# Second part of a hybrid decoder layer: VectorE sums for left operands, seven raw buffers for right operands

## The chip, the core and the metric

The kernel runs on one core of a Trainium2 chip. The metric is the device time of one execution in microseconds, as the median of several runs. The engines are called as in the profile: PE is TensorE's matmul, PEld its weight load, DVE is VectorE, ACT is ScalarE, POOL is GpSimd, SP is SyncE, which in this kernel issues most of the loads.

## The reference

One decoder layer on 2048 tokens of width 1024, with 16 meta tokens put in front. Two branches, a Mamba-2 scan and a gated linear attention, get their inputs from one projection, and two sigmoid gates merge them:

```python
u = rmsnorm(hres, norm_w)
proj = jnp.einsum('bld,dn->bln', u, w_in)
z, xbc, dt_raw, q, k, v, g_gla, a_lr, merge_g = split_cols(proj, IN_WIDTHS)
...
branches = jnp.stack([y_ssd.astype(y_gla.dtype), y_gla], axis=2)
branch_proj = jnp.einsum('blnc,ncd->blnd', branches, w_branch)
gates = jax.nn.sigmoid(merge_g.reshape(b, l, N_BRANCH, D_MODEL))
merged = jnp.sum(gates * branch_proj, axis=2)
return hres + jnp.einsum('bld,de->ble', merged, w_out)
...
return rmsnorm(h, final_norm_w)[:, N_META:]
```

All tensors are float32. The scans and their projections are the kernel's first part. The second part, which the change concerns, is the gates' projection (`merge_g`), the two branch projections and the output projection, with the final norm.

## The kernel before

*First part*, up to about 1487 us: projections, both scans, the branch outputs `y` and the normed input `u` go to DRAM in blocks.

*Second part*: seven stages, one after the other: gates of the first token block, its two branches, gates of the second block, its two branches, output. Each stage is a product of large matrices done by a Strassen-like scheme (Winograd's form): left and right matrices are cut in quarters, and seven products p = 1 to 7 stand for the eight of the plain way. The gate stages and the output have 8 left blocks n each (56 products), the branch stages 4 (28 products): 280 products in all.

A product (L1044 to L1060) is 12 matmuls of 128x512: four pieces j of the contraction, each done three times, since every operand is split into a high and a low half to keep float32 accuracy (lines L193 to L195: high by high and the two mixed ones). Products are written in the order p = 1, 2, 6, 7, 5, 3, 4, with two n interleaved, so that a pair of n makes a cycle of 14 products.

*Right operands* (28 per stage: 7 p times 4 j). `load_b` loads one from DRAM into a raw tile `br` of the pool `rawb`, which has five buffers, by a DMA on SP's queue (L1011). `prep_b` splits it: ACT copies the high half (L1016), DVE subtracts it to give the low half (L1017); these are the tiles `b`. Three of the seven are sums or differences of quarters that `make_sums` (L84) worked out earlier and stored to DRAM; those for the stages after the first gate stage are worked out inside the gate stages, in 64 instructions on POOL.

*Left operands*. `load_a` loads four quarters of each n into tiles `ar` (pool of eight, L1023 on SP's queue): three at one call, the fourth (a22) at a later call, 1.5 products on. At that call four additions and subtractions on POOL (L1031 to L1034) give the sums `as` and one new `ar`. `prep_a` splits each of the seven into tiles `a`: ACT at L1040, DVE at L1041.

*What a product leaves*. Three PSUM banks are kept going at once per n, named `psa`, `psb`, `psc`. The bank `psa` takes p = 1, 6, 5 and 3 in turn, each added to the last; after p = 1, 6 and 5 ACT copies the bank to a snapshot `sn` (L1057), and PE may not go on in that bank before the copy is done. Between p = 5 and p = 3 of one n lies only one product of the other n. A result is the bank, or a snapshot plus another bank (DVE, L1068). A gate stage then applies tanh (ACT, L1075) and stores; a branch stage multiplies with the gate on DVE and stores or adds in DRAM; the output stage adds the residual (DVE, L1117), squares (ACT, L1121) and, when a row is complete, takes the power -0.5 on POOL (L1129) and scales (DVE, L1132). Stores go by POOL's queue (L991).

*What sets the order*. A table `todo` holds, for each product's number, what is to be emitted after it: left loads 7.5 products before their first use, left splits 5 products before use, the splits of a stage's right operands 12 products ahead of its first product, then one each 0.8 products, and the loads 3.2 products ahead of their split. The order on PE and SP is that of the program. The order on ACT, DVE and POOL is set by a scheduler in the build, which works on a model of time. All queues are in order: an instruction that waits holds those behind it.

Of the kernel before, what the change touches and what calls it, by code (L numbers as in the profile page):

```python
# [7 lines left out]
F32 = mybir.dt.float32  # L8
# [4 lines left out]
ALU = mybir.AluOpType  # L13

P = 128
# [3 lines left out]
BLK = 512  # L19
# [21 lines left out]
def trunk_kernel(ctx: ExitStack, tc: tile.TileContext, xm, xmt, w_feat, w_tok, w_zm, w_br, w_o,  # L41
                 cf32, cmsk, pvec, fnw, hvec, gw2, out):
    nc = tc.nc
# [5 lines left out]
    def mk(pool, shape, dt, tag, **kw):  # L49
        cnt[0] += 1  # L50
        return pool.tile(shape, dt, tag=tag, name=f"{tag}_{cnt[0]}", **kw)
# [24 lines left out]
    def make_sums(pool, tag, nb, braw, sums, j, c, store):  # L76
        cs = slice(c * HB, (c + 1) * HB)
        pair = [mk(pool, [P, 512], F32, tag, bufs=nb).rearrange("p (i c) -> p i c", i=2) for _ in range(2)]
        for r, (k, t) in zip((t[:, i] for t in pair for i in range(2)), ((0, 1), (0, 0), (1, 1), (1, 0))):
            nc.sync.dma_start(r, braw(4 * k + j, t)[:, cs])  # L80
        yield
        (b12, b11), (b22, b21) = [(t[:, 0], t[:, 1]) for t in pair]
        for o, x, y in ((b11, b12, b11), (b12, b22, b12), (b22, b22, b11), (b21, b21, b22)):
            nc.gpsimd.tensor_tensor(o, x, y, op=ALU.subtract)  # L84
        if store is None:
            for dst, src in zip(sums, pair):
                late_store(dst[j][:, :, cs], src, 2)
            return
        yield
        yield  # L90
        for dst, src in zip(sums, pair):
            store.dma_start(dst[j][:, :, cs], src)
# [3 lines left out]
    def late_store(dst, src, lag=1):  # L96
        stores.setdefault(step_no[0] + lag, []).append((dst, src))
# [295 lines left out]
    def new_block(b, u):  # L393
        o = Block()
        o.b, o.u = b, u
        o.m0 = META if b == 0 else 0
        o.tt = o.m0 + BLK
        o.segs_all = [(0, o.tt // 2), (o.tt // 2, o.tt // 2)] if b == 0 else [(0, BLK)]
        o.segs_real = [(o.m0, BLK)]
        o.starts = [o.m0 + c * P for c in range(NCH)]  # L400
        o.chunks = ([(0, META)] if o.m0 else []) + [(a, P) for a in o.starts]
        o.ci0 = 1 if o.m0 else 0
        o.nck = len(o.chunks)
        for nm in ("tkd", "tkc", "ntc", "wde", "ecu", "dec"):
            setattr(o, nm, mk(bpool, [P, 5, NH], F32, nm, bufs=1))
        o.cumd = mk(dpool, [NH, BLK], F32, "cumd")
        o.g_all = mk(bpool, [P, GH, META + BLK], F32, "g_all")
        o.both = None
        if o.m0:
            o.both = mk(early, [P, KT, 2 * META], F32R, "both", bufs=1)  # L410
            for i in range(2):
                nc.gpsimd.tensor_copy(o.both[:, :, i * META:(i + 1) * META], u[i][:, :, :META].bitcast(F32))
        o.alr = mk(bpool, [P, 5, 48], F32, "alr")
        o.mov = lambda kt, a, n: tuple(t[:, kt, a:a + n] for t in u)
        return o
# [515 lines left out]
    def beside_unit(key):  # L931
        for j in range(4):
            for c in range(2):
                yield from make_sums(early, "wr", NWR, *sums[key], j, c, nc.sync)

    with tc.manual_schedule(engines={mybir.EngineType.PE, mybir.EngineType.SP}):
        for b in range(nblk):
            o = new_block(b, next_u[b])
# [25 lines left out]
    def pool2(name, bufs, **kw):  # L964
        return second.enter_context(tc.tile_pool(name=name, bufs=bufs, reuse_waits="tile", **kw))

    npl = pool2("rawb", 5)
# [4 lines left out]
    bpl = pool2("bops", 4)  # L972
    opl = pool2("outs", 1)
    spl = pool2("small", 4)
    pa = pool2("pa", 3, space=bass.MemoryType.PSUM)
    pc2 = pool2("pc2", 2, space=bass.MemoryType.PSUM)
    pb = pool2("pb", 3, space=bass.MemoryType.PSUM)
# [6 lines left out]
    store = late_store  # L984
# [11 lines left out]
    class Stage:  # L996
# [9 lines left out]
        def load_b(self, p, j):  # L1006
            src = {1: lambda j: self.braw(j, 0), 2: lambda j: self.braw(4 + j, 0), 3: lambda j: self.braw(4 + j, 1),
                   4: lambda j: self.sums[1][j][:, 1], 5: lambda j: self.sums[0][j][:, 1],
                   6: lambda j: self.sums[1][j][:, 0], 7: lambda j: self.sums[0][j][:, 0]}[p]
            raw = self.braws[p, j] = mk(npl, [P, BLK], F32, "br")  # L1010
            nc.sync.dma_start(raw, src(j))  # L1011

        def prep_b(self, p, j):
# [6 lines left out]
        def load_a(self, n):  # L1020
            def raw(i, j):
                t = mk(rpl, [P, 4, P], F32, "ar")
                nc.sync.dma_start(t, self.araw(n, i, j))  # L1023
                return t

            if n not in self.a:
                self.a[n] = raw(0, 0), raw(0, 1), raw(1, 0)
                return
            (a11, a12, a21), a22 = self.a[n], raw(1, 1)
            s1, s2, s4 = [mk(spl2, [P, 4, P], F32, "as") for _ in range(3)]  # L1030
            nc.gpsimd.tensor_tensor(s1, a21, a22, op=ALU.add)  # L1031
            nc.gpsimd.tensor_tensor(s2, s1, a11, op=ALU.subtract)
            nc.gpsimd.tensor_tensor(a21, a11, a21, op=ALU.subtract)
            nc.gpsimd.tensor_tensor(s4, a12, s2, op=ALU.subtract)  # L1034
            self.a[n] = {1: a11, 2: a12, 3: s4, 4: a22, 5: s1, 6: s2, 7: a21}

        def prep_a(self, n, p):
# [118 lines left out]
    def at(pos, fn):  # L1156
        pos = max(pos, -1)
        todo.setdefault(int(pos // 1), []).append((pos, len(todo), fn))
# [7 lines left out]
    for si, st in enumerate(stages):  # L1166
        for q in range(28):
            p, j = PS[q // 4], q % 4
            pos = begins[si] - 12 + 0.8 * q if si else -0.99 + 0.2 * (q // 4) if q < 16 else 2 * (q // 4 - 4)
            if si or p > 1:  # L1170
                at(pos - (3.2 if si else 0.1), lambda st=st, p=p, j=j: st.load_b(p, j))
            at(pos, lambda st=st, p=p, j=j: st.prep_b(p, j))
    for i, (st, n, p) in enumerate(order):
        if p in USES and st.fetch:
# [3 lines left out]
    begun_at = [begins[3 * s] for s in range(nsb)]  # L1178
    spots = [g + 9 + 5 * k for g in begun_at for k in range(8)]
    late_sums = [make_sums(opl, "io", 8, *sums[key], j, c, None) for key in late for j in range(4) for c in range(2)]  # L1180
    for pos, gen in zip(spots, late_sums):
        for k in range(2):
# [104 lines left out]
```

## Time and profile before

| | us |
|---|---|
| median of three runs | 2296.2 |
| the runs | 2296.17, 2296.2, 2300.63 |
| span of the profiled execution | 2298.3 |
| of this: PE busy | 2223.2 |
| DVE busy | 1646.5 |
| ACT busy | 1119.4 |
| POOL busy | 789.6 |
| second part, 1487 to 2298: PE busy | 774.0 |
| DVE, ACT, POOL busy there | 604.0, 395.4, 421.2 |

The profiled execution lies 2.1 us above the median. The stages of the second part begin at 1487.4, 1656.4, 1733.0, 1815.6, 1976.1, 2052.2 and 2130.7 us; the last product ends at 2286.8.

How to read the views that follow: in a row of the timeline stand start and length in us, engine, line, operation, tiles (out<-in), a count, and in brackets the time that the engine had been idle and what ended it. A row of waits gives the engine and line that waits, what it waits for, and us in total, times, longest. A row of a group gives busy us and mean ns, then idle time just before it.

### The profile page before, as it was taken

Reading aid. Unit: us, or ns where it says so; the run is one execution under the profiler, and the core shown is the slowest. Engines: PE = TensorE matmul, PEld = TensorE weight load, DVE = VectorE, ACT = ScalarE, POOL = GpSimd, SP = SyncE. Lnnn points to the kernel's source line nnn. Section 1 sums busy time; section 2 is a strip of 40 time slices with the busy share of each in tenths; the row PEclk is TensorE's granted clock in tenths of the full one; section 3 lists DMA queues with packets and bytes.
Section 4 is the critical chain, followed back from the end, with each engine's and each line's share of the span. In section 5 each row is a group of like instructions: output and inputs, shape, how many; then the busy total and the mean of one; then the engine's idle time right before and its main releaser. Section 6 shows DMA issues by size and latency. Waiting matters only on the chain.

```text
span 2298.3 us, 36496 instructions
## 1 busy us (share of the span) xinstructions
PE 2223.2 (97%) x12599; PEld 1938.7 (84%) x12599; DVE 1646.5 (72%) x3108; ACT 1119.4 (49%) x2508; POOL 789.6 (34%) x869
## 2 busy tenths in 40 slices
PE   6899999999999999999999999989999999999998
PEld 6899888888889889888988898868787788788786
DVE  5787767687765687775678656687778855788775
ACT  5565554463444454444445434554644545454443
POOL 3344533122221122212212100158535476535452
PEclk9999999999999999999999999999999999999999
DMA  7767866667886676886677654466767866679653
GB/s 254 232 221 245 296 211 208 211 193 246 267 264 208 205 225 208 272 278 206 203 215 230 215 184 149 149 221 205 264 233 223 249 216 213 233 251 252 182 185 110
DMA packets 281866, 507.51 MB, mean 221 GB/s; under 512 B 27104, under 2 KB 134880, under 8 KB 281680
## 3 DMA queue, kind: packets, MB, share of 16 engines
q1 hardware_dynamic: 217232, 413.76, 55.7%
q0 software_dynamic: 17568, 50.87, 7.3%
q10 hardware_dynamic: 46880, 40.54, 5.4%
q8 instruction: 99, 1.62, 0.3%
q14 instruction: 87, 0.71, 0.1%
HBM read 357.87 MB, written 147.19 MB: 220 GB/s over the span
## 4 chain that ended last, share of the span: by engine, by line
PE 73%; DVE 9%; DMA 9%; issue 4%; ACT 3%; POOL 2%; SPq 1%; ACTq 0%; POOLq 0%; DVEq 0%
PE pj L193 13%; PE pj L195 13%; PE pj L194 13%; PE psa L193 4%; PE psa L195 4%; PE psa L194 4%; DMA br<-br_t 2%; PE psb L195 2%; PE psb L193 2%; PE psb L194 2%; DVE b L1017 2%; PE pc L619 2%; PE pc L789 2%; PE pc L889 1%; PE pc L620 1%
## 5 line engine op out<-in xcount | busy, mean ns | idle before, releaser
L193 PE MATMUL pj<-u,whl 128*128 128x512 f32 (+1 forms) x1184 | 445.5, 376 | 9.4 <-ACT acc L529 4.5
L195 PE MATMUL pj<-u,whl 128*128 128x512 f32 (+1 forms) x1184 | 429.5, 363 | 0.0
L194 PE MATMUL pj<-u,whl 128*128 128x512 f32 (+1 forms) x1184 | 428.9, 362 | 0.0
L193 PE MATMUL pj<-whl,u 128*128 128x256 f32 (+1 forms) x992 | 288.8, 291 | 2.8 <-ACT u L261 2.2
L195 PE MATMUL pj<-whl,u 128*128 128x256 f32 (+1 forms) x992 | 282.4, 285 | 0.2 <-DVE u L266 0.2
L194 PE MATMUL pj<-whl,u 128*128 128x256 f32 (+1 forms) x992 | 282.1, 284 | 0.0
L193 PE MATMUL psa<-b,a 128*128 128x512 f32 x640 | 252.3, 394 | 18.1 <-ACT sn L1057 17.9
L193 PEld LDWEIGHTS pj<-u,whl 128*128 128x128 f32 x1184 | 223.6, 189 | 47.2 <-ACT acc L529 5.4
L195 PEld LDWEIGHTS pj<-u,whl 128*128 128x128 f32 x1184 | 223.2, 188 | 35.6
L194 PEld LDWEIGHTS pj<-u,whl 128*128 128x128 f32 x1184 | 223.9, 189 | 33.1
L194 PE MATMUL psa<-b,a 128*128 128x512 f32 x640 | 250.2, 391 | 0.9 <-DVE b L1017 0.9
L195 PE MATMUL psa<-b,a 128*128 128x512 f32 x640 | 250.5, 391 | 0.0
L84 POOL TENSOR_TENSOR wr<-wr 128x256 f32<-128x256 f32 x80 | 64.2, 803 | 428.8 <-DMA wr<-u 163.4
L181 POOL TENSOR_TENSOR whl<-wr,whl 128x512 fp32r<-128x512 f32 (+1 forms) x100 | 138.3, 1389 | 187.2 <-ACT whl L180 154.8
L1041 DVE TENSOR_TENSOR a<-ar,a 128x512 fp32r<-128x512 f32 x160 | 157.3, 993 | 61.9 <-ACT a L1040 61.4
L1017 DVE TENSOR_TENSOR b<-br,b 128x512 fp32r<-128x512 f32 x196 | 159.1, 833 | 49.1 <-ACT b L1016 48.8
L193 PEld LDWEIGHTS pj<-whl,u 128*128 128x128 f32 x992 | 189.8, 191 | 4.5 <-ACT u L261 2.3
L195 PEld LDWEIGHTS pj<-whl,u 128*128 128x128 f32 x992 | 189.8, 191 | 0.8 <-DVE u L266 0.8
L194 PEld LDWEIGHTS pj<-whl,u 128*128 128x128 f32 x992 | 189.9, 191 | 0.4
L1016 ACT ACTIVATE b<-br 128x512 fp32r<-128x512 f32 x196 | 120.1, 628 | 125.2 <-DMA br<-br_t 53.6
L533 DVE SCALAR_TENSOR_TENSOR acc<-cin,hcw,acc 128x512 f32<-128x512 f32 (+1 forms) x192 | 161.3, 840 | 11.4 <-ACT acc L529 9.3
L193 PEld LDWEIGHTS psa<-b,a 128*128 128x128 f32 x640 | 120.9, 189 | 49.3 <-ACT sn L1057 24.7
(297 smaller groups left out, 5064.5 us busy)
## 6 DMA issues: line engine op xcount, KB each, us to landing
whl<-k_s SPq DMA_DIRECT2D x96, 512.0 KB, 4.4
whl<-k_g SPq DMA_DIRECT2D x96, 512.0 KB, 4.2
whl<-k_v SPq DMA_DIRECT2D x48, 512.0 KB, 4.0
whl<-k_z SPq DMA_DIRECT2D x36, 512.0 KB, 4.1
wr<-in_w_feat SPq DMA_DIRECT2D x64, 256.0 KB, 4.4
k_s<-whl SPq DMA_DIRECT2D x32, 512.0 KB, 3.8
cb<-cumd ACTq DMA_DIRECT2D x64, 256.0 KB, 5.8
k_g<-whl SPq DMA_DIRECT2D x32, 512.0 KB, 3.8
```

The source lines that it names most:

```text
L84: nc.gpsimd.tensor_tensor(o, x, y, op=ALU.subtract)
L181: nc.gpsimd.tensor_tensor(hl[:, 1], raw, hl[:, 0].bitcast(F32), op=ALU.subtract)
L193: nc.tensor.matmul(ps, sh, mh, start=first, stop=False, **kw)
L194: nc.tensor.matmul(ps, sh, ml, start=False, stop=False, **kw)
L195: nc.tensor.matmul(ps, sl, mh, start=False, stop=last, **kw)
L533: nc.vector.scalar_tensor_tensor(acc, cin[:, k:k + tt], hcw[:, ti, k:k + 1], acc, op0=ALU.mult, op1=ALU.add)
L619: nc.tensor.matmul(py[:, h * 64:(h + 1) * 64], dm[:, h], xdt[:, h], start=True, stop=True)
L620: nc.tensor.matmul(py[:, 256:512], cf[:, a:a + P], s_ssd[:, g], start=True, stop=True)
L789: nc.tensor.matmul(ps[:, r * P:(r + 1) * P], kq[:, 2 * r * P:(2 * r + 1) * P], kq[:, (2 * r + 1) * P:(2 * r + 2) * P], start=True, stop=True)
L1016: nc.scalar.activation(t[:, 0], raw, AF.Copy)
L1017: nc.vector.tensor_tensor(t[:, 1], raw, t[:, 0].bitcast(F32), op=ALU.subtract)
L1041: nc.vector.tensor_tensor(t[:, 1], src, t[:, 0].bitcast(F32), op=ALU.subtract)
```

## The change

Three edits, all in the second part. The four sums of `load_a` and the 64 late differences of `make_sums` (where `store is None`) move from POOL to DVE. The pool of raw right operands becomes a ring of seven, as a second pool of two stands beside the five. And the loads of right operands are emitted 4.8 products ahead of their split, not 3.2. Lines from L974 on move by 6 in the changed file (the sums L1031 to L1034 are L1037 to L1040 there, the DVE splits L1023 and L1047, the copies L1063, the adds L1074).

```diff
-            nc.gpsimd.tensor_tensor(o, x, y, op=ALU.subtract)
+            (nc.vector if store is None else nc.gpsimd).tensor_tensor(o, x, y, op=ALU.subtract)
...
+    npl2 = pool2("rawb2", 2)
+    taken = [0]
+
+    def raw_b():
+        taken[0] += 1
+        return mk(npl2 if taken[0] % 7 > 4 else npl, [P, BLK], F32, "br")
...
-            raw = self.braws[p, j] = mk(npl, [P, BLK], F32, "br")
+            raw = self.braws[p, j] = raw_b()
             nc.sync.dma_start(raw, src(j))
...
-            nc.gpsimd.tensor_tensor(s1, a21, a22, op=ALU.add)
-            nc.gpsimd.tensor_tensor(s2, s1, a11, op=ALU.subtract)
-            nc.gpsimd.tensor_tensor(a21, a11, a21, op=ALU.subtract)
-            nc.gpsimd.tensor_tensor(s4, a12, s2, op=ALU.subtract)
+            nc.vector.tensor_tensor(s1, a21, a22, op=ALU.add)
+            nc.vector.tensor_tensor(s2, s1, a11, op=ALU.subtract)
+            nc.vector.tensor_tensor(a21, a11, a21, op=ALU.subtract)
+            nc.vector.tensor_tensor(s4, a12, s2, op=ALU.subtract)
...
-                at(pos - (3.2 if si else 0.1), lambda st=st, p=p, j=j: st.load_b(p, j))
+                at(pos - (4.8 if si else 0.1), lambda st=st, p=p, j=j: st.load_b(p, j))
```

DVE has 224 instructions more and POOL 224 fewer; the counts on the other engines stay. The order of the first part is the same on every engine.

On SP, at the end of the second gate stage (about 1945 us; `br` are raw right operands of the next stage, `ar` left quarters), the order before:

```order
L1011 DMA br_21448<-br_t_3_196 128x512
L1023 DMA ar_21466<-in_w_br 128x512
L1011 DMA br_21481<-br_t_0_189 128x512
L1023 DMA ar_21483<-in_w_br 128x512
L1023 DMA ar_21485<-in_w_br 128x512
L1023 DMA ar_21487<-in_w_br 128x512
L1023 DMA ar_21506<-in_w_br 128x512
L1011 DMA br_21521<-br_t_1_190 128x512
L1011 DMA br_21541<-br_t_2_191 128x512
L1011 DMA br_21549<-br_t_3_192 128x512
```

and now:

```order
L1017 DMA br_21420<-br_t_3_196 128x512
L1029 DMA ar_21425<-in_w_br 128x512
L1029 DMA ar_21427<-in_w_br 128x512
L1029 DMA ar_21429<-in_w_br 128x512
L1017 DMA br_21431<-br_t_0_189 128x512
L1017 DMA br_21455<-br_t_1_190 128x512
L1029 DMA ar_21473<-in_w_br 128x512
L1017 DMA br_21485<-br_t_2_191 128x512
L1029 DMA ar_21490<-in_w_br 128x512
L1029 DMA ar_21492<-in_w_br 128x512
L1029 DMA ar_21494<-in_w_br 128x512
L1029 DMA ar_21513<-in_w_br 128x512
```

The right operands br_t_1_190 and br_t_2_191 stand ahead of the last four left quarters, where they stood behind them.

On ACT, at the end of the first branch stage (about 1722 us; L1016, now L1022, are splits of right operands, L1057, now L1063, the copies of a bank after p = 5 of two n), the order before:

```order
L1040 ACTIVATE a_19377<-ar_19056 128x512
L1040 ACTIVATE a_19419<-ar_19316 128x512
L1016 ACTIVATE b_3396_19473<-br_19380 128x512
L1057 ACTIVATE sn_19362<-psa_19151 128x512
L1040 ACTIVATE a_19448<-ar_19385 128x512
L1016 ACTIVATE b_3400_19498<-br_19425 128x512
L1057 ACTIVATE sn_19403<-psa_19174 128x512
```

and now:

```order
L1046 ACTIVATE a_19384<-ar_19059 128x512
L1022 ACTIVATE b_3398_19480<-br_19332 128x512
L1022 ACTIVATE b_3401_19503<-br_19355 128x512
L1046 ACTIVATE a_19426<-ar_19323 128x512
L1022 ACTIVATE b_3405_19528<-br_19390 128x512
L1063 ACTIVATE sn_19369<-psa_19158 128x512
L1046 ACTIVATE a_19455<-ar_19392 128x512
L1022 ACTIVATE b_3409_19549<-br_19432 128x512
L1063 ACTIVATE sn_19410<-psa_19181 128x512
```

Each copy stands behind two later splits of right operands than before.

On DVE, in the first gate stage (about 1563 us; L1068, now L1074, is the add of a snapshot and a bank), the order before:

```order
L1041 TENSOR_TENSOR a_17973<-ar_17683,a_17973 128x512
L1041 TENSOR_TENSOR a_18010<-ar_17922,a_18010 128x512
L1068 TENSOR_TENSOR sn_17960<-sn_17960,psb_17906 128x512
L1041 TENSOR_TENSOR a_18028<-ar_17976,a_18028 128x512
L1068 TENSOR_TENSOR sn_17994<-sn_17994,psb_17928 128x512
```

and now:

```order
L1047 TENSOR_TENSOR a_17976<-ar_17686,a_17976 128x512
L1047 TENSOR_TENSOR a_18013<-ar_17925,a_18013 128x512
L1037 TENSOR_TENSOR as_18006<-ar_17983,ar_18004 128x512
L1038 TENSOR_TENSOR as_18007<-as_18006,ar_17979 128x512
L1039 TENSOR_TENSOR ar_17983<-ar_17979,ar_17983 128x512
L1040 TENSOR_TENSOR as_18008<-ar_17981,as_18007 128x512
L1074 TENSOR_TENSOR sn_17963<-sn_17963,psb_17909 128x512
L1047 TENSOR_TENSOR a_18031<-ar_17979,a_18031 128x512
L1074 TENSOR_TENSOR sn_17997<-sn_17997,psb_17931 128x512
```

The four sums, of which the first reads the fourth quarter (ar_18004), stand between the splits and the add.

## The prediction

> **What bounds the kernel now.** I read the busy times by stretch of the second part first, then the waits there, then one stall in three timelines. In the stretches the columns are: length, then busy time and count of PE, PEld, DVE, ACT and POOL, granted clock, DMA share, GB/s.
>
> ```profile
> 1487.00:1580.00 93.00, 83.91 (x362) 67.45 (x361) 75.39 (x76) 51.30 (x97) 57.30 (x61) 0.96 0.65 217
> 1640.00:1700.00 60.00, 57.75 (x254) 47.17 (x253) 44.49 (x57) 30.23 (x54) 29.84 (x29) 1.00 0.65 226
> 1700.00:1760.00 60.00, 59.13 (x259) 47.97 (x258) 51.38 (x65) 32.18 (x58) 24.39 (x22) 1.00 0.78 255
> 1760.00:1820.00 60.00, 57.15 (x244) 46.51 (x243) 49.08 (x62) 25.90 (x46) 30.04 (x25) 0.97 0.86 237
> 1940.00:2000.00 60.00, 54.31 (x233) 44.41 (x232) 43.01 (x55) 32.10 (x59) 22.71 (x22) 0.97 0.72 241
> 2000.00:2060.00 60.00, 60.00 (x267) 49.65 (x266) 49.30 (x63) 29.10 (x51) 25.64 (x24) 1.00 0.72 247
> 2120.00:2180.00 60.00, 55.56 (x243) 45.03 (x242) 48.57 (x69) 29.60 (x60) 28.40 (x26) 1.00 0.69 194
> ```
>
> TensorE is the bound: a full stretch holds 267 matmuls in 60 us, one every 0.2247 us, and a product of 12 takes 2.7 us. Only fewer gaps can shorten the part; the change touches no matmul. The stretches from 1640, 1700, 1760, 1940 and 2120 lack 13, 8, 23, 34 and 24 matmuls, 102 in all or 23 us; each holds the end of one stage and the start of the next. The first stretch could hold 93 / 0.2247 = 414 and has 362: 11.7 us at the start. Together some 35 us, which is the most that this change can win.
>
> ```profile
> PE psa L193 <- ACT sn L1057: 17.9, 13, 5.7
> PE psc L194 <- DVE b L1017: 6.7, 2, 4.0
> ACT b L1016 <- DMA br<-br_t: 53.6, 32, 6.7
> ACT b L1016 <- DMA br<-gate_t: 27.6, 18, 4.2
> ACT b L1016 <- DMA br<-out_t: 19.2, 9, 6.3
> ```
>
> These are the waits (total us, times, longest). At stage ends PE waits for no operand: it waits for ACT's copy of a PSUM bank (L1057), because the same bank must take the next product (p=3 after p=5 of the other n, one product later). ACT in turn stands in front of raw right operands that are not there, 100 us over those three rows. One such stall (SP's queue, then ACT, then PE):
>
> ```profile
> 1946.83 11.21 SPq L1023 DMA_DIRECT2D ar<-in_w_br  x4
> 1958.10 2.32 SPq L1011 DMA_DIRECT2D br<-br_t  x5
> ...
> 1961.67 1.30 ACT L1016 ACTIVATE b<-br 128x512 fp32r<-128x512 f32 x2 [6.73 <-DMA br<-br_t]
> 1962.87 0.58 ACT L1057 ACTIVATE sn<-psa 128x512 f32<-128x512 f32 x1
> ...
> 1957.43 0.39 PE L195 MATMUL psa<-b,a 128*128 128x512 f32 x1
> 1963.51 0.80 PE L193 MATMUL psa<-b,a 128*128 128x512 f32 x1 [5.69 <-ACT sn L1057]
> ```
>
> SP stands 11.2 us in four left loads, issues the right loads behind them at 1958.1, ACT gets data at 1961.7, its copy comes behind the splits, PE has lost 5.69 us. The splits themselves belong to the next stage and are wanted far later; what hurts is that the copy queues behind them.
>
> Why were SP's left loads held? By slots that DVE's splits free, and DVE is slow wherever POOL computes:
>
> ```profile
> L1017 DVE TENSOR_TENSOR b<-br,b x196: 677/686/5074, 1326.7 to 2149.5; 128x512 fp32r<-128x512 f32 x196
> L1041 DVE TENSOR_TENSOR a<-ar,a x160: 676/693/2664, 1487.9 to 2268.5; 128x512 fp32r<-128x512 f32 x160
> L1041 DVE TENSOR_TENSOR a<-as,a x120: 678/692/7537, 1493.3 to 2263.8; 128x512 fp32r<-128x512 f32 x120
> ...
> L1017 DVE TENSOR_TENSOR b<-br,b 128x512 fp32r<-128x512 f32 x196 | 159.1, 833 | 49.1 <-ACT b L1016 48.8
> L1041 DVE TENSOR_TENSOR a<-ar,a 128x512 fp32r<-128x512 f32 x160 | 157.3, 993 | 61.9 <-ACT a L1040 61.4
> L1041 DVE TENSOR_TENSOR a<-as,a 128x512 fp32r<-128x512 f32 x120 | 125.7, 1048 | 37.7 <-ACT a L1040 36.8
> ```
>
> Minimum, median and maximum ns stand first, then busy us and mean ns. By median the 476 splits would take 134.5 + 110.9 + 83.0 = 328.4 us; they take 442.1. DVE loses 114 us, in single instructions of up to 7.5 us.
>
> **The change part by part.** *Sums of left operands to DVE*: 160 instructions, and the 64 late differences (L84). Their price on POOL, and the nearest price on DVE (equal tile, all f32; 128x256 from the first part; two DVE instructions in a row, 0.60 us apart):
>
> ```profile
> L1031 POOL TENSOR_TENSOR as<-ar,ar 128x512 f32<-128x512 f32 x40 | 59.0, 1476 | 122.9 <-DMA ar<-m 30.7 <-DMA ar<-in_w_br 30.5 <-DMA ar<-in_w_feat 17.9
> L633 DVE TENSOR_TENSOR tok<-c,tok x64: 409/425/1481, 109.4 to 1348.8; 128x256 f32<-128x256 f32 x64
> 2186.68 0.68 DVE L1041 TENSOR_TENSOR a<-as,a 128x512 fp32r<-128x512 f32 x1
> 2187.28 0.69 DVE L1117 SCALAR_TENSOR_TENSOR io<-sn,io 128x512 f32<-128x512 f32 x1
> ```
>
> DVE gains 160 × 0.60 = 96 us and 64 × 0.425 = 27 us, 123 in all, and can win back at most the 114. Its load rises by 9 us at the least and by 123 if nothing comes back; I take the even end, since the minimum and the median of the splits lie within 16 ns, so the slow ones are the exception that needs POOL. None of this is on PE's path by itself: DVE is busy 42 to 51 of 60 us in the quoted stretches. What matters is that the long single instructions go, and with them SP's long stands.
>
> What the long ones cost at the start is on PE's path:
>
> ```profile
> 1496.03 9.08 DVE L1017 TENSOR_TENSOR b<-br,b 128x512 fp32r<-128x512 f32 x6
> 1502.77 0.79 PE L194 MATMUL psc<-b,a 128*128 128x512 f32 x1 [4.03 <-DVE b L1017]
> 1512.18 0.50 PE L194 MATMUL psa<-b,a 128*128 128x512 f32 x1 [0.93 <-DVE b L1017]
> ```
>
> Six splits in 9.08 us where six at 0.60 take 3.7; PE waits for them 6.7 us in all (the row of psc among the waits), its next matmuls take longer, and at 1512 it waits for one more. But in the new order DVE does the eight sums of the first two pairs (8 × 0.60 = 4.8 us) between them. So 4.8 of some 5.4 us goes back here: the last of these splits comes about 0.6 us earlier, and the first product a little later. The wait at 1512 comes from the same slow splits, and goes with what follows from it. I take 4.5 us of the 12 (bounds 0 and 9).
>
> *Seven raw buffers, loads 4.8 products ahead*: each right load moves 1.6 products, 4.3 us, ahead of its split. On SP it is moved past left loads: the order at the 1946 stall shows two right loads more in front of the four left loads. No DMA is added; SP issues one in about 0.45 us (2.32 us for five). In the stall above data landed 3.6 us after the issue, and ACT was 6.73 us late for it; a load that is issued ahead of the 11.21-us stand is there in time. Of the other stage ends the largest single stall is shorter than the 4.3 us that the loads gain:
>
> ```profile
> 1805.66 0.50 PE L193 MATMUL psa<-b,a 128*128 128x512 f32 x1 [2.54 <-ACT sn L1057]
> ```
>
>  Two things speak against winning all: the changed ACT order puts the copies one or two splits further back (b00→b10: two splits more stand ahead of the p=5 copies), so an ACT that must wait for a load now waits for a later one; and four of seven buffers would have to be free early, which needs DVE. Since the left loads are held 3 to 6 us less once the 7-us splits are gone, 3 of the 23 us at stage ends stay (bounds 0 and 20).
>
> *New wait*: DVE is in order, so where a sum waits for its fourth quarter (L1029's last load), all behind it wait: splits, and the adds (L1074 in the new file) that precede ACT's tanh and the next copy. On POOL the same wait held only stores:
>
> ```profile
> POOL as L1031 <- DMA ar<-m: 30.7, 5, 9.3
> POOL as L1031 <- DMA ar<-in_w_br: 30.5, 7, 8.1
> POOL as L1031 <- DMA ar<-in_w_feat: 17.9, 5, 6.3
> ...
> 2192.68 1.48 POOL L1031 TENSOR_TENSOR as<-ar,ar 128x512 f32<-128x512 f32 x1 [6.88 <-DMA ar<-m]
> ```
>
> In the last stage DVE comes to this sum after its instruction at 2187.28 and would stand to 2192.5, some 5 us. Left operands are split several products before use, so most such stands cover themselves; one us of PE is my figure there. In gate stages the four sums stand ahead of the add:
>
> ```profile
> 1556.11 6.69 DVE L1041 TENSOR_TENSOR a<-as,a 128x512 fp32r<-128x512 f32 x1 [0.83 <-ACT a L1040]
> 1569.08 1.30 POOL L1031 TENSOR_TENSOR as<-ar,ar 128x512 f32<-128x512 f32 x1 [4.87 <-DVE a L1041]
> 1567.14 0.58 ACT L1057 ACTIVATE sn<-psa 128x512 f32<-128x512 f32 x1
> 1569.22 0.39 PE L193 MATMUL psa<-b,a 128*128 128x512 f32 x1
> ```
>
> With data at 1569.0, four sums (2.4), add, tanh (0.6 each) and copy would end at 1573.2 in place of 1567.7: PE takes the bank at 1569.2, so 4 us are lost. But that data was late because its slot waited for a split behind the 6.69-us instruction; at 0.69 us it lands 6 us sooner, and the loss is nothing. Over all 40 pairs I take 2.5 us (bounds 0, and 10 for the three worst places at 4, 4 and 2).
>
> The sum: lost before 12 + 23 = 35; after, 7.5 + 3 + 2.5 = 13. That is 22 won; I take 20 since an ACT order that is worse by two splits will not be the only surprise. The profiled execution spans 2298.3 us, 2.1 above the median of 2296.2: 2278.3, less 2.1, is **2276**.
>
> **A rule against it.** The Trainium skill, "Perfetto Trace Analysis", section "Optimizing Scalar/DVE Operations", says that GpSimd and DVE share a port, which a two-port DVE instruction holds exclusively, "so offloading operations between those two might not help". The means above agree that they hurt one another: 114 us of splits. By that rule the move is neutral and only the buffers count; its result stands as rival C.
>
> **The rivals.**
> A. *The extra lead is eaten.* ACT's copies stand behind later splits, whose loads are still behind left loads: stage ends keep 20 of 23 us. For: the order on ACT. Against: the left loads' stand of 11.21 us came from slow splits. Losses 7.5 + 20 + 2.5 = 30, won 5: **2291**.
> B. *Slower: DVE stands before late left quarters.* In the eight-pair gate stages and the last stage the add and the copy come behind the sum. It decides where the quarter lands later than the add's turn by over 1.5 us. For: 79 us of such waits in the three POOL rows. Against: they came to a POOL which was there early, and the slow splits that made them go. With the three places at 10 us, the start unchanged and stage ends keeping all 23 and losing 4 more under DVE's added 123 us: 12 + 10 + 27 = 49 against 35, 14 lost at worst; half of that, **2303**.
> C. *Moving the sums is neutral* (DVE's own time for them uses up what it no longer loses): start keeps 12, new waits 2.5, stage ends keep 5 by the buffers alone: 19.5, won 15.5, **2281**. For: 123 against 114 us. Against: an even load is not a 7-us instruction in the wrong place.
> D. *The buffers do nothing*, since each ring slot is freed by a DVE split and seven slots fill as five did: stage ends keep 12 by the faster splits alone, 7.5 + 2.5 + 12 = 22, won 13: **2283**.
>
> **How the numbers follow.** Chances: forecast 0.5 (own range 2264 to 2285), A 0.2, B 0.12, C 0.1, D 0.08. The best case is bounded by 2296 − 35 = 2261. A range of **2264 to 2294** leaves out B's upper part and a little of A. A measurement of this kernel can tell about 0.2%, 4.6 us: faster means under 2291.6. Forecast, C and D lie under it, with half of A and hardly any of B: 0.5 + 0.18 + 0.1 = 0.78. Same: half of A and some of B, 0.12. Slower, over 2300.8: 0.10.
>
> **What would show it.** Right: in the stretches 1640, 1760, 1940 and 2120 of the new profile PE holds 260 or more matmuls; the wait of PE for ACT's copy falls from 17.9 to under 6 us; DVE's splits have means near 700 ns and none over 2 us; POOL has no tensor work but the power of the last stage. The first stretch shows 375 or more. Wrong: ACT's waits for raw right operands still 60 us or more with copies behind them (A); PE waiting for ACT's copy in mid-stage, behind an add behind a sum which waited for a left load (B); start and stage ends improved by the buffers with splits still slow (C); SP standing in right loads on DVE splits as before (D).

## The result, and the profile after

| | before | changed |
|---|---|---|
| median, us | 2297.4 (2296.2 to 2300.6, 4 runs) | 2277.5 (2274.8 to 2278.6, 4 runs) |
| ratio, 95% interval | | 0.9904 (0.9888 to 0.9921) |
| span of the profiled execution | 2298.3 | 2275.6 |

The change wins 20 us, 1%. The profiles differ by 22.7 us, as the profiled execution of before is on the slow side of its runs (a span is some 1.8 us shorter than the time of the same execution: 2275.6 for 2277.34). In a second comparison, further down, the changed kernel stands at 0.9894 (0.9879 to 0.9909).

The same stretches of the changed kernel, with the columns as before (length, busy time and count of PE, PEld, DVE, ACT, POOL, granted clock, DMA share, GB/s):

```profile
1487.00:1580.00 93.00, 86.92 (x377) 69.27 (x377) 72.55 (x127) 53.41 (x99) 19.65 (x31) 0.98 0.72 242
1640.00:1700.00 60.00, 59.33 (x262) 48.84 (x261) 46.06 (x74) 30.51 (x55) 7.57 (x14) 1.00 0.65 226
1760.00:1820.00 60.00, 59.52 (x263) 48.97 (x262) 48.77 (x80) 32.63 (x58) 11.21 (x13) 1.00 0.90 239
1940.00:2000.00 60.00, 60.00 (x266) 49.56 (x265) 45.53 (x72) 29.67 (x53) 7.55 (x14) 1.00 0.70 248
2120.00:2180.00 60.00, 60.00 (x267) 49.70 (x266) 43.34 (x76) 26.46 (x57) 9.13 (x14) 1.00 0.57 174
```

The stage ends, where 13, 23, 34 and 24 matmuls were missing, are nearly full; the start has 377 of 414. PE's waits, and ACT's for raw right operands, in the second part:

```profile
PE psa L193 <- ACT sn L1063: 4.1, 4, 2.2
PE psc L194 <- DVE b L1023: 3.1, 4, 1.6
ACT b L1022 <- DMA br<-br_t: 19.8, 19, 2.2
ACT b L1022 <- DMA br<-gate_t: 17.3, 12, 3.6
ACT b L1022 <- DMA br<-out_t: 11.3, 7, 3.3
```

PE waits 4.1 us for ACT's copies where it waited 17.9, and ACT 48 us for those right operands where it waited 100. The place of the 5.69-us stall, on SP and then on ACT (PE comes to this place 10 us earlier here, since less was lost up to there):

```profile
1934.84 6.20 SPq L1029 DMA_DIRECT2D ar<-in_w_br  x4
1941.10 2.65 SPq L1017 DMA_DIRECT2D br<-br_t  x5
...
1944.71 0.60 ACT L1063 ACTIVATE sn<-psa 128x512 f32<-128x512 f32 x1 [0.79 <-PE psa L195]
```

SP still stands in four left loads, but two more right operands were issued ahead of them, and ACT's copy waits only for PE. And DVE's splits (minimum, median, maximum ns) have lost their tail:

```profile
L1023 DVE TENSOR_TENSOR b<-br,b x196: 682/686/700, 1327.9 to 2120.0; 128x512 fp32r<-128x512 f32 x196
L1047 DVE TENSOR_TENSOR a<-ar,a x160: 680/691/699, 1488.9 to 2245.7; 128x512 fp32r<-128x512 f32 x160
L1047 DVE TENSOR_TENSOR a<-as,a x120: 681/692/700, 1496.9 to 2242.3; 128x512 fp32r<-128x512 f32 x120
```

So both things that were forecast are seen, and every sign that the prediction listed as "right" with them. But both edits are in this kernel, so the signs can't tell the forecast from rival C, in which only the buffers count. Whether both brought time is what the runs below ask.

### The profile page after: what moved, and what is told of

It reads as the page before. It is cut to its first block, busy times and chain, and to the rows that moved or that the text cites. A ratio compares the mean times of both kernels' runs of the same rounds, so it can differ in the third digit from the quotient of the medians.

```text
span 2275.6 us, 36414 instructions
## 1 busy us (share of the span) xinstructions
PE 2216.7 (97%) x12599; PEld 1936.4 (85%) x12599; DVE 1626.3 (71%) x3332; ACT 1119.0 (49%) x2508; POOL 511.8 (22%) x645
## 4 chain that ended last, share of the span: by engine, by line
PE 79%; DVE 8%; DMA 5%; issue 3%; ACT 3%; POOL 1%; SPq 1%; ACTq 0%; POOLq 0%; DVEq 0%
PE pj L193 13%; PE pj L195 12%; PE pj L194 12%; PE psa L193 6%; PE psa L194 6%; PE psa L195 6%; PE psb L194 3%; PE psb L193 3%; PE psb L195 3%; PE pc L619 2%; PE pc L789 2%; PE psc L194 1%; PE psc L193 1%; PE psc L195 1%; PE pc L620 1%
## 5 line engine op out<-in xcount | busy, mean ns | idle before, releaser
L533 DVE SCALAR_TENSOR_TENSOR acc<-cin,hcw,acc 128x512 f32<-128x512 f32 (+1 forms) x192 | 160.4, 835 | 13.1 <-ACT acc L529 10.9
L1047 DVE TENSOR_TENSOR a<-ar,a 128x512 fp32r<-128x512 f32 x160 | 109.9, 690 | 82.0 <-ACT a L1046 81.3
L84 POOL TENSOR_TENSOR wr<-wr 128x256 f32<-128x256 f32 x80 | 72.3, 904 | 423.0 <-DMA wr<-u 159.9
L1022 ACT ACTIVATE b<-br 128x512 fp32r<-128x512 f32 x196 | 118.3, 626 | 58.2 <-DMA br<-br_t 19.8
L193 PEld LDWEIGHTS psa<-b,a 128*128 128x128 f32 x640 | 120.2, 188 | 31.2 <-ACT sn L1063 6.2
L195 PEld LDWEIGHTS psa<-b,a 128*128 128x128 f32 x640 | 120.2, 188 | 26.4 <-DVE a L1047 1.4
```

Source lines behind the costliest of these rows:

```text
L84: (nc.vector if store is None else nc.gpsimd).tensor_tensor(o, x, y, op=ALU.subtract)
L193: nc.tensor.matmul(ps, sh, mh, start=first, stop=False, **kw)
L195: nc.tensor.matmul(ps, sl, mh, start=False, stop=last, **kw)
L533: nc.vector.scalar_tensor_tensor(acc, cin[:, k:k + tt], hcw[:, ti, k:k + 1], acc, op0=ALU.mult, op1=ALU.add)
L1022: nc.scalar.activation(t[:, 0], raw, AF.Copy)
L1047: nc.vector.tensor_tensor(t[:, 1], src, t[:, 0].bitcast(F32), op=ALU.subtract)
```

## The experiments

One number is worked out in the same way from every trace: the time that PE lost. It is the sum, from 1480 us to the last product, of the distances between the starts of consecutive matmuls as far as they exceed 0.227 us, split at 1540 us into the start and what comes later (stage ends above all). A row is one profiled execution; most lie within 4 us of their median, that of "lead only" 6.4 us above it. Each ratio is against runs of the kernel before that were taken together with it.

| kernel | buffers, lead | sums on | ratio to before (95%) | lost at start | lost later |
|---|---|---|---|---|---|
| before | 5, 3.2 | POOL | 1 | 13.0 | 23.8 |
| changed | 7, 4.8 | DVE | 0.9904 (0.9888 to 0.9921) | 10.2 | 2.9 |
| changed, again | 7, 4.8 | DVE | 0.9894 (0.9879 to 0.9909) | 8.7 | 2.3 |
| sums only | 5, 3.2 | DVE | 0.9945 (0.9927 to 0.9964) | 11.4 | 11.3 |
| buffers and lead | 7, 4.8 | POOL | 0.9906 (0.9887 to 0.9926) | 11.2 | 4.0 |
| seven only | 7, 3.2 | POOL | 0.9941 (0.9928 to 0.9955) | 9.2 | 14.1 |
| lead only | 5, 4.8 | POOL | 0.9950 (0.9936 to 0.9963) | 13.4 | 13.5 |

Not all of this is waiting. Before, three of the longest waits are followed by some eight matmuls that start 0.43 us apart in place of 0.227, with a granted clock of 0.5 there (from 1499.0, 1806.2 and 1963.2 us); that is 4.7 us of the lost time. The changed kernel loses 1.0 us so (from 1500.9), and 2.7 in its second profile: 2 to 4 of the 20 us won are matmuls that no longer run at half the clock.

**The sums alone.** The changed kernel without the second pool and with the old lead:

```diff
-        return mk(npl2 if taken[0] % 7 > 4 else npl, [P, BLK], F32, "br")
+        return mk(npl, [P, BLK], F32, "br")
...
-                at(pos - (4.8 if si else 0.1), lambda st=st, p=p, j=j: st.load_b(p, j))
+                at(pos - (3.2 if si else 0.1), lambda st=st, p=p, j=j: st.load_b(p, j))
```

> The sums of left operands and the late differences on DVE, with five raw buffers and loads 3.2 products ahead. Theory T (both causes act in series at a stage end: slow splits hold SP, and the small ring gives no slack): the start is that of the changed kernel (about 3 us better), stage ends lose 8 to 12 of their 23 us: ratio 0.9935 to 0.9955. Rival S (the sums alone, the ring is not needed): stage ends lose 3 us, ratio 0.991 or lower. Rival B (the buffers alone): only the start improves, ratio 0.998 to 0.9995. In all three DVE's splits have means near 690 ns.

Measured: 0.9945 (0.9927 to 0.9964), 2285.1 us. This is theory T's number; rival B, which left the stage ends as they were, falls here. Half of what the stage ends lost stays lost, though no split is slow any more. At the place of the 5.69-us stall (SP, then ACT):

```profile
1937.80 8.14 SPq L1029 DMA_DIRECT2D ar<-in_w_br  x4
1945.99 2.33 SPq L1017 DMA_DIRECT2D br<-br_t  x5
...
1949.91 0.63 ACT L1022 ACTIVATE b<-br 128x512 fp32r<-128x512 f32 x1 [4.39 <-DMA br<-br_t]
```

SP stands 8.1 us in left loads with fast splits, and ACT still comes 4.39 us too early for a right operand that was issued behind them.

**The buffers and the lead alone.** All sums on POOL, as before (one of the four lines is shown):

```diff
-            nc.vector.tensor_tensor(s1, a21, a22, op=ALU.add)
+            nc.gpsimd.tensor_tensor(s1, a21, a22, op=ALU.add)
...
-            (nc.vector if store is None else nc.gpsimd).tensor_tensor(o, x, y, op=ALU.subtract)
+            nc.gpsimd.tensor_tensor(o, x, y, op=ALU.subtract)
```

> Seven raw buffers and loads 4.8 products ahead, with all sums on POOL as before. Theory T: start unchanged (15 us lost), stage ends lose about 10 of 23 us: ratio 0.993 to 0.9955. Rival B: stage ends lose 3 us or less, ratio 0.991 to 0.992. Rival S: ratio 0.998 to 1.000, as the ring's slots are still freed by slow splits. DVE's splits have means of 830 to 1050 ns in all three.

Measured: 0.9906 (0.9887 to 0.9926), 2277.3 us: what rival B has for this kernel, and theory T not. This is the changed kernel's time without the moved sums, and the slow splits are all there (minimum, median, maximum ns of DVE's splits):

```profile
L1023 DVE TENSOR_TENSOR b<-br,b x196: 675/683/5061, 1327.9 to 2122.9; 128x512 fp32r<-128x512 f32 x196
L1047 DVE TENSOR_TENSOR a<-ar,a x160: 675/693/7814, 1487.8 to 2246.6; 128x512 fp32r<-128x512 f32 x160
```

while two of its stretches at stage ends, with the columns as before, are full:

```profile
1640.00:1700.00 60.00, 60.00 (x266) 49.73 (x265) 49.35 (x61) 31.00 (x56) 28.08 (x28) 1.00 0.67 231
1940.00:2000.00 60.00, 59.78 (x263) 48.86 (x262) 44.48 (x56) 28.75 (x53) 32.52 (x30) 1.00 0.70 244
```

Single splits take 5 and 7.8 us, and at the stage ends PE hardly notices. At the start it does: it waits 6.7 us for low halves of the second product's right operand, as before. Theory T, that both causes act in series, is wrong in this direction: either part takes away half or more of the loss at stage ends by itself, and beside the buffers the sums are worth no more than these runs can tell, some 4 us.

SP's waits for left slots from 1530 us on say why (total us, times, longest). Before:

```profile
SPq L1023 <- DVE a L1041: 183.7, 46, 16.4
```

with the sums alone moved:

```profile
SPq L1029 <- DVE a L1047: 172.5, 42, 13.2
```

with the buffers and the lead alone:

```profile
SPq L1029 <- DVE a L1047: 187.7, 49, 12.8
```

and in the changed kernel:

```profile
SPq L1029 <- DVE a L1047: 179.5, 45, 13.2
```

SP stands some 180 us before left loads in all four, slow splits or not. (Where the sums are on DVE, the views put 36 us more of such stands down to DVE's late differences, L84.) With eight buffers that are filled 7.5 products ahead, I read these stands as the pace at which PE uses left operands up, not as lateness of DVE; no run varied that pace. What a right load then needs is to be in front of them in SP's queue.

**The number of buffers, and the lead, each alone** (sums on POOL in both; the first keeps 3.2, the second keeps five; the edits are against the kernel with buffers and lead alone).

```diff
-                at(pos - (4.8 if si else 0.1), lambda st=st, p=p, j=j: st.load_b(p, j))
+                at(pos - (3.2 if si else 0.1), lambda st=st, p=p, j=j: st.load_b(p, j))
```

> Sums on POOL, seven raw buffers, loads 3.2 products ahead of the split (four loads of 0.8 products in flight by the table). Theory L (the lead alone puts right loads in front of the left loads in which SP stands; the ring must only be long enough for it): five buffers were enough for 3.2, so nothing changes: ratio 0.998 to 1.000. Rival R (the ring is what matters: SP stood in right loads for a free slot, and seven slots end that): ratio 0.991 to 0.995.

```diff
-        return mk(npl2 if taken[0] % 7 > 4 else npl, [P, BLK], F32, "br")
+        return mk(npl, [P, BLK], F32, "br")
```

> Sums on POOL, five raw buffers, loads 4.8 products ahead of the split (six in flight by the table, so the ring caps it at five). Theory L: right loads go in front of the left ones, but SP then stands in them for a slot; about half of the gain: ratio 0.993 to 0.997. Rival R: nothing, or a loss, as SP's stand for a slot now holds left loads too: ratio 0.999 to 1.004.

Measured: 0.9941 (0.9928 to 0.9955) for the seven, 0.9950 (0.9936 to 0.9963) for the lead. Each gives a little more than half of the 0.9906 of both, so the two gains nearly add up; theory L fails on the first, rival R on the second. SP's waits from 1487 us on, for right and for left slots, with seven buffers at 3.2:

```profile
SPq L1029 <- DVE a L1047: 215.9, 58, 13.2
SPq L1017 <- DVE b L1023: 171.8, 74, 16.6
```

and with five at 4.8:

```profile
SPq L1017 <- DVE b L1023: 220.2, 109, 16.1
SPq L1029 <- DVE a L1047: 160.7, 41, 14.5
```

The lead moves the stand from the left loads to the right ones; seven slots move it back. With both it is 188.5 us for right slots and 187.7 for left, and the kernel before has 211.2 and 183.7: the totals of the two, 376 to 395 us in these kernels, differ too little to tell them apart. PE's wait for ACT's copies does follow the time lost later: 17.9 us before, 9.5 with seven buffers, 11.2 with the lead, 2.2 with both. Which loads are late in front of which copies with one of the two alone was not traced, so why each gives about half stays open.

**POOL's work put back, without its sums.** The changed kernel, with POOL multiplying the fourth sum by one, four times:

```diff
+    one = mk(spl, [P, 1, 1], F32, "one", bufs=1)
+    nc.vector.memset(one, 1.0)
...
             nc.vector.tensor_tensor(s4, a12, s2, op=ALU.subtract)
+            for _ in range(4):
+                nc.gpsimd.tensor_tensor(s4, s4, one.to_broadcast([P, 4, P]), op=ALU.mult)
```

> The changed kernel, and behind each group of four sums POOL multiplies the tile of the fourth sum by one, four times: 160 instructions of 128x512 on POOL that change no value and that nothing needs for 8 products or more. Theory T (DVE's splits are slow because POOL works at the same time, whatever POOL does): splits have means of 850 ns or more with single ones over 3 us, the sums on DVE are slowed too, and 5 to 15 us come back: ratio to the kernel before 0.994 to 0.998. Rival (the sums' own place and their dependences were what hurt, not POOL's work): means stay near 690 ns and the ratio stays at 0.990 to 0.991.

Measured: 1.0054 (1.0033 to 1.0075), 2309.9 us, slower than before, where theory T had 0.998 at the most; 16.0 us are lost at the start and 29.4 later. The groups (busy us and mean ns behind the bar):

```profile
L1044 POOL TENSOR_TENSOR as<-as,one 128x512 f32<-128x512 f32 x160 | 202.9, 1268 | 216.7 <-DVE as L1042 199.0 <-ACT sn L1085 11.0
L1051 DVE TENSOR_TENSOR a<-ar,a 128x512 fp32r<-128x512 f32 x160 | 144.3, 909 | 47.9 <-ACT a L1050 47.6
L1025 DVE TENSOR_TENSOR b<-br,b 128x512 fp32r<-128x512 f32 x196 | 139.8, 744 | 2.9 <-ACT b L1024 2.7
L1040 DVE TENSOR_TENSOR as<-as,ar 128x512 f32<-128x512 f32 x40 | 33.3, 834 | 0.7
```

DVE's instructions become slow again, the moved sums too (from 689 to 834 ns in one line), and nothing but 2.9 us of ACT waits for POOL's tiles: POOL's work does slow DVE, also when it is of no use. But the means are smaller than before the change, the mean of the right splits (744 ns) and the longest single split (2.4 us) stay below what theory T had, and the time is worse. The kernel with the buffers alone has as many instructions of this size on POOL and stands at 0.9906. Two things differ: DVE's own load, 1716.7 us busy here and 1654.0 there, and the sums in DVE's order. PE waits 18.0 us for ACT's copies. Of its eleven longest stalls after the start, six are of the stage-end kind again, a copy behind a right operand that is late, in spite of seven buffers (2.9 us at 2143). Two are rival B's chain of the prediction, 2.8 us at 1848 and this one (DVE, then ACT, then PE):

```profile
2234.66 0.69 DVE L1039 TENSOR_TENSOR as<-ar,ar 128x512 f32<-128x512 f32 x1 [5.28 <-DMA ar<-m]
2235.26 0.68 DVE L1127 SCALAR_TENSOR_TENSOR io<-sn,io 128x512 f32<-128x512 f32 x1
...
2236.06 0.63 ACT L1131 ACTIVATE junk<-io 128x512 bf16<-128x512 f32 x1 [5.92 <-DVE io L1127]
2236.69 0.58 ACT L1067 ACTIVATE sn<-psa 128x512 f32<-128x512 f32 x1
...
2237.32 0.50 PE L193 MATMUL psa<-b,a 128*128 128x512 f32 x1 [3.65 <-ACT sn L1067]
```

A sum stands 5.28 us before its late quarter, the residual's add stands behind the sum, ACT behind the add, and the copy that PE needs behind that. That a slow DVE costs time only where it has no room left would fit both kernels, but no run varied DVE's load alone, and the scheduler set another order too: why this kernel is slower than the one before stays open in part.

**The start: four attempts.** Three theories on the 10.2 us that the changed kernel loses there (the expectations say 12 or 12.5; the sum as told above gives 10.2). First, the second product's right operand is loaded ahead of the left quarters (the line that then leaves out its later load is not shown):

```diff
-    for j in range(4):
-        at(-1, lambda j=j: stages[0].load_b(1, j))
+    for p in (1, 2):
+        for j in range(4):
+            at(-1, lambda p=p, j=j: stages[0].load_b(p, j))
```

> The changed kernel, with the four loads of the second product's right operand in front of the first left loads, so that they do not wait until 1489 us on SP. Theory T (the start's 12.5 us are lost to low halves of that operand which come late, since their loads come late): the waits of psc for DVE go, 5 to 9 us are won over the changed kernel, ratio to the kernel before 0.9865 to 0.9885. Rival (DVE's work at the start is the bound: splits and sums of the first pairs have to be done at any rate): the wait moves to the left splits, under 3 us won, ratio 0.989 to 0.991.

Measured: 0.9902 (0.9882 to 0.9922), nothing won; 10.2 us lost at the start. The wait went to the left operands: SP's queue and PE's wait,

```profile
1473.55 1.74 SPq L1017 DMA_DIRECT2D br<-u  x4
1475.34 19.23 SPq L1029 DMA_DIRECT2D ar<-in_w_feat  x8
...
1497.37 0.80 PE L193 MATMUL psa<-b,a 128*128 128x512 f32 x1 [6.01 <-ACT a L1046]
```

The third of these left loads was issued at 1491.02, as a store of `y` from ACT's queue had landed at 1491.00; in the changed kernel the second right load was issued at 1489.44, that store's landing being 1489.42. In both cases the trace gives the store and the load the same completion semaphore, which the load waits for (number 100 in this kernel, 104 in the changed one). So the stores of `y` went to POOL's queue next:

```diff
-            nc.scalar.dma_start(y_left[1][o.b][2 * h + j], got["gs"][j])
+            (nc.gpsimd if o.b == nblk - 1 and h == GH - 2 else nc.scalar).dma_start(
+                y_left[1][o.b][2 * h + j], got["gs"][j])
```

> The changed kernel, with the last two stores of y by ACT's queue (near 1487 us) moved to POOL's queue. Theory Q (at the start SP stands from 1474 to 1489 us since the load's completion counter is one that ACT's store of y holds until it lands at 1489.4): the stand goes, the second product's right operand lands before 1482, and 5 to 9 us of the start's 12.5 are won: ratio to the kernel before 0.9865 to 0.989. Rival D (the start is bound by DVE and ACT, which finish the first part and then have some 25 instructions to do): under 2 us won, ratio 0.990 to 0.991.

> As the last, but on the kernel with seven buffers and lead 4.8 and all sums on POOL. Theory Q: 5 to 9 us won over that kernel (0.9906): ratio 0.987 to 0.989. Rival D: ratio 0.990 to 0.991. If the sums on DVE are worth something at the start, it stays 1 to 3 us behind the run before.

The stand is gone in the first of them:

```profile
1461.63 8.21 SPq L1029 DMA_DIRECT2D ar<-in_w_feat  x7
1469.94 1.80 SPq L1017 DMA_DIRECT2D br<-u  x4
```

These four had landed by 1476.8; those of the changed kernel landed between 1478.3 and 1495.2. Yet the ratios are 0.9899 (0.9885 to 0.9914) and 0.9908 (0.9895 to 0.9922): rival D in both. The second, with the sums on POOL, stays 1.9 us behind the first, as its expectation allows, but the intervals overlap. In the first PE still waits 2.7 us for low halves of that operand, which DVE splits at its place in the order, behind sums. Last, then, the order: the fourth quarter of the first two n is loaded later, so that the scheduler puts the sums behind the splits, with the stores of `y` on POOL as well:

```diff
-            at(i - LOAD + 1.5, lambda st=st, n=n: st.load_a(n))
+            at(i - LOAD + 1.5 if i > 1 else -0.7, lambda st=st, n=n: st.load_a(n))
```

(-0.56 in the second, which is behind the operand of p = 6 too; `load_a` keeps the first three quarters apart till then.)

> The changed kernel with the last two stores of y on POOL's queue, and with the fourth left quarter of the first two n loaded behind the second product's right operand, so that the first eight sums come behind its splits in DVE's order. Theory O (the start is lost because DVE does sums ahead of the splits that PE waits for; loads are no longer what is late): PE's waits for the low halves of the second product go, 5 to 9 us of the start's 12 are won: ratio to the kernel before 0.9865 to 0.9885. Rival W (DVE and ACT have more work at the start than fits, whatever its order): the wait moves to the third product, under 3 us won: 0.989 to 0.991.

> As the run before, with that fourth quarter loaded behind the right operand of p = 6 as well, so that the sums come behind those splits too. Theory O: the same, within 2 us, or worse if the left sums for p = 6 are late then. Rival W: 0.989 to 0.992.

> As the first of these, with all sums on POOL. If the sums on DVE are worth nothing beside the buffers, this equals the first within 2 us. If POOL's sums at the start slow the splits (six splits in 9 us in the kernel before), it stays 3 to 6 us behind the first.

> The changed kernel itself, on the same chip as these runs: ratio 0.990 to 0.991.

Measured on one chip: 0.9909 (0.9896 to 0.9923), 0.9899 (0.9884 to 0.9914), 0.9945 (0.9933 to 0.9958) and, for the changed kernel itself, 0.9894 (0.9879 to 0.9909). Theory O falls: the waits for the second product go, and others come a few products on, as rival W had it. In the first of the four:

```profile
1499.34 0.50 PE L194 MATMUL psc<-b,a 128*128 128x512 f32 x1 [0.29 <-DVE b L1023]
1505.36 0.50 PE L195 MATMUL psa<-b,a 128*128 128x512 f32 x1 [0.88 <-DVE a L1048]
1510.78 0.50 PE L193 MATMUL psa<-b,a 128*128 128x512 f32 x1 [2.86 <-ACT a L1047]
1513.19 0.80 PE L195 MATMUL psa<-b,a 128*128 128x512 f32 x1 [1.68 <-DVE a L1048]
```

In the third, with the sums on POOL, the start loses 19.4 us, against 11.8 in the first. DVE's row there, and the wait it makes:

```profile
1497.19 7.66 DVE L1023 TENSOR_TENSOR b<-br,b 128x512 fp32r<-128x512 f32 x3
...
1504.30 0.80 PE L194 MATMUL psc<-b,a 128*128 128x512 f32 x1 [4.50 <-DVE b L1023]
```

Three splits in 7.66 us: with this order, and at this place, where DVE is what PE waits for, the sums on DVE are worth 8 us (2279.4 against 2287.2). None of these kernels is faster than the changed one beyond its interval.

## Why the prediction was right, and where it was wrong

The forecast, 2276, was 1.5 us from the median, and the gain of 20 is the one that was forecast. The interval of the ratio is 4 us to either side, so that it came so close is luck. Its steps, one by one:

*The stage ends.* Predicted: 3 of 23 us stay; measured 2.9 and 2.3 in two profiles. The chain that was read (right loads behind left ones on SP, ACT in front of a missing operand, the copy behind it, PE) was the right one, and the buffers and the lead alone undo it: ACT's waits for those operands fall from 100 to 44 us and PE's for the copies from 17.9 to 2.2. Rival D, for which the buffers do nothing, falls with this. The price of the changed ACT order, which the same step allowed for, is in those 2 to 3 us at most.

*What did it.* Wrong step: "What matters is that the long single instructions go, and with them SP's long stands." The long instructions went, and SP's stands before left loads stayed (183.7 us before, 179.5 after; the longest 16.4 and 13.2). With the slow splits kept, the buffers and the lead alone give 0.9906 against 0.9904, and 4.0 us lost later. So the reason that the prediction gave for its 3 us, left loads that are held 3 to 6 us less, was not needed. Rival C had this result at 2281, with 5 us kept at stage ends by the buffers alone; its mechanism is the nearer one, with a measured 2277. The single 11.21-us stand that I quoted was shorter with fast splits (8.1 us with the sums alone, 6.2 with all), but a stand matters only by what is queued behind it.

*The even account on DVE.* Predicted: +123 us, -114. The sums take 686 to 691 ns each and in a row start 0.61 us apart, L84 takes 422 ns, all close to the price, and the splits came down to their medians. DVE's whole busy time went from 1646.5 to 1626.3 us, 20 less, not 9 more: other lines of DVE had been slowed as well, above all the product with the gates, which came down from 1042 to 686 ns, 17 us over its 48 instructions. The prediction counted the splits alone.

*The rule against the move.* The Trainium skill ("Perfetto Trace Analysis", section "Optimizing Scalar/DVE Operations") says that moving work between these two might not help. The runs agree in the version with the buffers (0.9906 without the move, 0.9904 and 0.9894 with it), and not where the buffers were left out (the move alone gave 0.9945), nor at the start with the later fourth quarter (0.9909 with the move, 0.9945 without).

*The start.* Predicted 4.5 us won of 12; the profiles give 2.8 and 4.3 of 13.0, with the sums alone 1.6, and with the buffers alone 1.8, so this too can't be put down to the sums by these profiles. The term was right in size. That the sums give most of it back by their place in DVE's order was right for what PE waits for first, but moving them behind the splits won nothing: the work is only waited for later.

*The new waits.* Predicted 2.5 us in all, and seen once, in the first profile: PE waits 2.23 us at 1529 for a copy behind a tanh behind an add behind four sums (DVE, then ACT, then PE),

```profile
1524.76 0.69 DVE L1037 TENSOR_TENSOR as<-ar,ar 128x512 f32<-128x512 f32 x1 [0.65 <-DMA ar<-in_w_feat]
1527.31 0.68 DVE L1074 TENSOR_TENSOR sn<-sn,psb 128x512 f32<-128x512 f32 x1
...
1528.02 0.63 ACT L1081 ACTIVATE sn<-sn 128x512 f32<-128x512 f32 x1 [1.96 <-DVE sn L1074]
1528.56 0.58 ACT L1063 ACTIVATE sn<-psa 128x512 f32<-128x512 f32 x1
...
1529.19 0.50 PE L193 MATMUL psa<-b,a 128*128 128x512 f32 x1 [2.23 <-ACT sn L1063]
```

That is rival B's chain, at the start and for 2 us. It is not in the second profile of the same kernel. DVE stands 40 us before late quarters in the second part, and what PE loses later on, 2.9 and 2.3 us, lies mostly at stage ends. So the term was about right, with fast splits; with POOL's work put back the same chain costs more.

*The sum* was 35 lost before and 13 after; the traces give 36.8 and 13.1 or 11.0. The right total came from terms of which one, the sums' part in the stage ends, was credited to the wrong edit: right in number and in what PE waits for, but not in which edit ends the wait.

## What to carry to other kernels

Where two edits come together and each has a mechanism in the trace, run each alone before one is believed: here the more visible fault, single instructions of 7 us, was worth no more than the runs can tell once the quieter one, late loads of right operands, was mended. A sign that both theories share does not choose between them. A long stand of a queue before a full ring may be only the pace of the consumer; ask what is queued behind it. Ring length and lead each gave a little more than half alone, and nearly the sum together.

## What the runs showed of the hardware that was not expected

POOL's tensor work slows DVE's by single instructions, not evenly: medians of the splits stay at 682 to 693 ns with and without it, while the longest goes from 700 to 7814 ns. Work on POOL that computes nothing new does it as well, up to 2.4 us. Not every line is hit: before the change, with the buffers alone and with POOL's work put back, no DVE instruction of the second part that reads one tile from PSUM and one from SBUF (L1068, and L1094 and L1117 with `psa`) took more than 692 ns, while L1094 and L1117 with two SBUF tiles have single ones of 1.5 to 2.2 us. The scaling L1132 is not hit either (754 ns at most); whether POOL worked beside it was not looked into.

Loads on SP's queue near 1474 us stood for 15 us until a store from ACT's queue had landed (issued at 1489.44, the store's landing 1489.42; in another kernel 1491.02 and 1491.00), and stood no more when that store went by POOL's queue. In both kernels store and load have the same completion semaphore in the trace, 104 and 100, and the load waits for it: the two queues share it.
